# A decoder block on one core: seven block products for three quarters of the second MLP product, and another order of the first values

## The chip, the cores and the metric

The kernel runs on one core of one Trainium2 chip. The metric is the device time of one execution in microseconds, the median of several runs. A profile comes from one further execution, taken by the hardware profiler.

The engines are named as in the profile: PE is TensorE's matmul, PEld its weight load, DVE is VectorE, ACT is ScalarE, POOL is GpSimd, and SP is SyncE, whose queue issues nearly all DMAs of this kernel, in program order.

## The reference, cut to what matters

One decoder block over 1024 tokens of width 1024: a token mixer (retention and dilated attention), then an MLP. Both are behind an RMS norm that is modulated by a conditioning vector, and a last RMS norm follows. All values are fp32.

```
mod = silu(c) @ w_ada + b_ada;  sh1, sc1, g1, sh2, sc2, g2 = split(mod, 6)
h = rms_norm(x, norm1_g) * (1 + sc1) + sh1
x = x + g1 * token_mixer(h, ...)
h = rms_norm(x, norm2_g) * (1 + sc2) + sh2
x = x + g2 * (square(relu(h @ w_ff1)) @ w_ff2)          # 1024 -> 4096 -> 1024
out = rms_norm(x, norm_f_g)
```

The change touches the last line but one, in its second product (`w_ff2`, 4096 x 1024), and the first use of `h`, in the first projection of the token mixer (the attention values, `w_av`).

## The kernel before

Features stand on the 128 partitions and tokens in the free dimension. `x1` is eight tiles of 128 x 1024 (`G["x1", f]`), and the squared activations of the MLP are 32 such tiles, called `a` here and `a_d` in DRAM.

**Numbers.** Each fp32 operand is split into a high part, rounded to fp32r by ScalarE, and a low part, the difference, by VectorE. A product of two such pairs is three matmuls of 128 x 128 by 128 x 512 (`mm3`, lines 193, 195 and 197).

**Steps.** The class `Steps` (line 55) keeps a list of bodies, each with the weight tiles that it loads. Three raw buffers (tag `raw`) are loaded ahead on SP; `split_w` (line 180) makes the high and low parts into the tags `wh` and `wl`, three buffers each. A step that isn't `manual` has the weights of the next steps prepared ahead of its body; a manual one calls `ahead(...)` where it wants that. Loads beyond a mark wait for `first["release"]()`. The order of instructions on each engine is the order of the program.

**The first values.** `av_first` (line 768) runs over the eight k-tiles of `h`. PE needs `hh[k]` and `hl[k]`, the high and low parts. They come from `xt[k]` by VectorE's scaling (`h1_scale`, line 456), ScalarE's `hh` (line 458) and VectorE's `hl` (`h1_low`, line 461); ahead of the scaling, two rows of `w_ada` are multiplied with the condition on VectorE (`mod1`, line 433). One weight tile serves two k-tiles; for an even k, `ahead(1)` stands between the scaling and `mod1`, and has ScalarE round the next weight (line 183) and VectorE subtract (line 184). `split_first` (line 759) keeps the subtraction back in a list, to be called later; it was used for the first weight only.

**The first MLP product.** `ff1` (line 1642) makes 16 column blocks q of 256 features each by seven products for eight (class `Blocks`, line 212, items in the order 11, s1, s3, s2, 12, 22, s4, 12 matmuls each). Weight sums and splits (`prep`) run ahead as far as there are free slots: four of tag `g1` and four of `att` are used once, then four of `att` and six of `wh` and `wl` in turn. `post` forms the outputs on VectorE, and `f_out` (line 1609) applies relu and square on ScalarE and stores two tiles of `a` per block to DRAM (line 1622).

**The second MLP product.** `ff2(c, j)` (line 1759) runs over seven chunks c of four k-tiles each (512 of the 4096 features), and within a chunk over four weight tiles j. Each step does two column tiles f, each with two token halves: 24 matmuls into two PSUM banks. VectorE then adds the result, times the gate, to `x1` (line 1768). The k-tiles of `a` come back from DRAM through the raw buffers and are split ahead of their chunk (`a_prep`, lines 1754 and 1755). The eighth chunk is `ff2_last` (line 1785), in three runs over tokens, with the last norm and the output woven in. `x1` itself is loaded back from DRAM during the last column block of `ff1` and just behind it (`x1_load`, line 1508).

Of the kernel before, what the change touches and what calls it, by code (L numbers as in the profile page):

```python
# [11 lines left out]
F32 = mybir.dt.float32  # L12
F32R = mybir.dt.float32r
# [4 lines left out]
P = 128  # L18
# [114 lines left out]
def block_kernel(ctx, tc, io, stop=None, dbg=None):  # L133
# [34 lines left out]
    a1 = cst.tile([P, NK], F32, name="a1")  # L168
    a2 = cst.tile([P, NK], F32, name="a2")
    dsh = cst.tile([P, NK // 2], F32, name="dsh")  # L170
    ident = ct[:, CS_ID:CS_ID + P]
    ones = ct[:, CS_ONE:CS_ONE + 1]
    mhalf = ct[:, CS_MH:CS_MH + 8]
# [552 lines left out]
    def wsplit(ap):  # L726
        return ap, split_w
# [40 lines left out]
    def av_first(kk):  # L768

        def body(ahead, w):  # L770
            for k in (2 * kk, 2 * kk + 1):
                if k == 0:
                    for j, rb in enumerate(first["rb"]):
                        nc.scalar.copy(rb1[:, 512 * j:512 * j + 512], rb)
                if k + 1 < NK:
                    h1_mods(k + 1)
                    h1_scale(k + 1)
                    if k % 2 == 0:
                        ahead(1)
                    if k + 2 < NK:  # L780
                        mod1(k + 2)
                    h1_low(k + 1)
                av_k(0, k, w)
                if k == 3:
                    first["release"]()
                if k == 4:
                    for g in range(3):
                        bias_out(g)
                if k == NK - 1:
                    ahead(1)  # L790
                    nc.sync.dma_start(cs, io["cossin"])
                    nc.sync.dma_start(decay, io["decay"])
        return body
# [146 lines left out]
        new_head(0)  # L940

    for kk in range(4):
        steps.add(av_first(kk), [(io["w_av"][kk], split_w if kk else split_first)], manual=True)
    for g in (1, 2):
        for kk in range(4):
            steps.add(av_step(g, kk), [wsplit(io["w_av"][4 * g + kk])])
    steps.mark()
    steps.add(queries_keys, manual=True)

# [631 lines left out]

    M = {}
    NQ = DFF // 256
    a_d = [dram.tile([P, S], F32, name=f"ad{t}") for t in range(2 * NQ)]
    def w1_load(q, part):

        if q < 2:
# [21 lines left out]
    def f_out(q, n, x, y=None):  # L1609

        if ("out", q) not in M:
            M["out", q] = [G["p"].tile([P, S], F32, tag="g0", bufs=8, name=f"a{2 * q + i}") for i in range(2)]
        i, t = int(n[0]) - 1, int(n[1]) - 1
        o = M["out", q][i][:, 512 * t:512 * t + 512]
        if y is None:
            nc.scalar.activation(o, x, AF.Relu)
        else:
            (nc.vector.tensor_add if n == "12" else nc.vector.tensor_sub)(o, x, y)  # L1618
            nc.scalar.activation(o, o, AF.Relu)  # L1619
        nc.scalar.activation(o, o, AF.Square)  # L1620
        if n in ("12", "21"):
            nc.sync.dma_start(a_d[2 * q + i], M["out", q][i])
# [19 lines left out]
    def ff1(ahead):  # L1642
        def t_(k, half):
            return G["x1", k][:, 512 * half:512 * half + 512]

        def norm(k):
            t = t_(k, 1)
            nc.vector.scalar_tensor_tensor(t, t, a2[:, k:k + 1], G["rb"], op0=ALU.mult, op1=ALU.mult)

        banks(True)  # L1650

        BF.mm(0, "11", range(3))
        G["rs"] = rstd_rows(G["acc", "n21"], "n21", G["mp"], lambda: BF.prep((2, "11"), (2, "s1")))
# [60 lines left out]
        BF.post(1, "s2")  # L1714
        low()
        low = t4(2)
        l = t4(3)
        low()
        l()
        for k in range(NK):  # L1720
            del G["x1", k]
        for q in (3, 4):
            for part in (1, 2):
                w1_load(q, part)
        for q in range(2):
            BF.post(q, "12")
        sums = [(q, n) for q in range(2, NQ) for n in ORDER]
        items = [(q, n) for n in ("s4", "22") for q in range(2)] + sums

        def before(q, n):  # L1730
            if q == NQ - 2 and n == "s4":
                first["release"]()
            if q > 2 and n == ORDER[0] and q + 2 < NQ:
                for part in (1, 2):
                    w1_load(q + 2, part)
            if q == NQ - 1 and n in ("s2", "12"):
                for f in range(3):
                    x1_load(f + 3 * (n == "12"), x1_d)

        def after(q, n):  # L1740
# [5 lines left out]
        x1_load(7, x1_d)  # L1746

    def a_prep(t):

        def prep(raw):  # L1750
            pool, tag = ((G["p"], "g1"), (A["r1"], "att"))[t // 4 % 2]
            hi = pool.tile([P, S], F32R, tag=tag, bufs=8, name=f"a{t}h")
            lo = pool.tile([P, S], F32R, tag=tag, bufs=8, name=f"a{t}l")
# [89 lines left out]

    nff = DFF // P
    steps.add(ff1, manual=True)
    behind = [(a_d[t], a_prep(t)) for t in range(4)]
    for c in range(7):
        for j in range(4):
            steps.add(ff2(c, j), [wsplit(io["w_ff2"][4 * c + j])] + behind)
            behind = [(a_d[4 * c + 4 + j], a_prep(4 * c + 4 + j))]  # L1850
    for r in range(3):
        for j in range(4):
            steps.add(ff2_last(r, j), behind + [(io["w_ff2"][28 + j], last_prep(j))] if r == 0 else [])
            behind = []

    steps.run(startup)
# [17 lines left out]
def _k4(w):  # L1874

    k = w.shape[0]
    t = w.reshape(k // 512, 4, P, 4, 2, P).transpose(0, 3, 2, 4, 1, 5)
    return np.ascontiguousarray(t).reshape(k // 512 * 4, P, 1024)

def _vcols(w, width):  # L1880

# [44 lines left out]
def pack(x, c, w_ada, b_ada, norm1_g, w_in, rel_bias, ret_gn_g, ret_gn_b,  # L1926
# [27 lines left out]
        "w_ff2": _k4(A(w_ff2)[0]),  # L1954
    }
    a.update(_constants())
    return a
# [17 lines left out]
```

## Time and profile before

| | before |
|---|---|
| median of 3 runs | 2317.35 us (2315.91 to 2317.53) |
| the profiled execution | 2316.94 us |
| its span, first to last instruction | 2315.0 us |
| PE busy | 2261.9 us, 98%, 10466 matmuls |
| VectorE busy | 1350.1 us, 58% |
| ScalarE busy | 808.2 us, 35% |
| mean granted clock of PE | 0.998 |
| moved by DMA | 274.65 MB, mean 119 GB/s |

The profiled execution lies 0.41 us below the median, and its time is 1.94 us longer than its span. In the order of the span, the first values run from about 23 to 78 us, `ff1` from about 1626 to 1946, the seven chunks of `ff2` to about 2257, and the last chunk with the output to 2315. Matmuls are pipelined, so one has a duration of some 0.39 us while the next starts 0.23 us later; paces are therefore taken from start to start.

### The profile page before, as it was taken

How to read it: one execution, taken by the hardware profiler on the slowest of the kernel's cores; microseconds unless marked ns; L12 is line 12 of the kernel's file. 1: busy time of each engine (PE TensorE's matmuls, PEld its weight loads, DVE VectorE, ACT ScalarE, POOL GpSimd, SP SyncE). 2: the span in 40 equal slices, each digit the busy share in tenths (PEclk: the TensorE clock that was granted, in tenths of full speed). 3: DMA queues.
4: the chain of work that ended last, by engine and by line, in shares of the span. 5: the costliest groups of instructions: out<-in, count | busy, mean ns of one | idle time of the engine just before them, and what ended most of it. 6: DMA issues, size and time to landing. Idle time of an engine off the chain costs nothing.

```text
span 2315.0 us, 26666 instructions
## 1 busy us (share of the span) xinstructions
PE 2261.9 (98%) x10466; PEld 1864.6 (81%) x10466; DVE 1350.1 (58%) x1986; ACT 808.2 (35%) x1479; POOL 171.7 (7%) x136
## 2 busy tenths in 40 slices
PE   6999999999999999999999999999999999999998
PEld 4787888888878787888788888888778887888887
DVE  5626555547677676855555646567855554544445
ACT  3324233222334343444535411134454444221112
POOL 0000000001101010100000014401000000000003
PEclk9999999999999999999999999999999999999999
DMA  8532333332323232233323353253223336323222
GB/s 350 192 127 99 115 114 110 110 133 104 118 86 126 89 119 91 83 130 102 96 72 96 136 174 97 90 189 118 68 108 109 109 108 218 111 91 103 98 82 73
DMA packets 101661, 274.65 MB, mean 119 GB/s; under 512 B 22423, under 2 KB 33950, under 8 KB 101407
## 3 DMA queue, kind: packets, MB, share of 16 engines
q1 hardware_dynamic: 100382, 270.85, 34.1%
q0 software_dynamic: 1152, 2.10, 0.3%
q8 instruction: 82, 1.34, 0.2%
q14 instruction: 45, 0.36, 0.1%
HBM read 208.27 MB, written 67.00 MB: 119 GB/s over the span
## 4 chain that ended last, share of the span: by engine, by line
PE 57%; DVE 5%; ACT 3%; DMA 1%; issue 1%; POOLq 0%; SPq 0%; POOL 0%; DVEq 0%; ACTq 0%
PE f L193 4%; PE f L197 4%; PE f L195 4%; PE fp L193 4%; PE fp L197 4%; PE fp L195 4%; PE ro L195 3%; PE ro L193 3%; PE ro L197 3%; PE ak L193 2%; PE ak L195 2%; PE ak L197 2%; PE rg L195 1%; PE rg L193 1%; PE wo L193 1%; PE wo L195 1%
## 5 line engine op out<-in xcount | busy, mean ns | idle before, releaser
L1768 DVE SCALAR_TENSOR_TENSOR x1r<-f,mods,x1r 128x512 f32<-128x512 f32 x112 | 78.7, 746 | 153.4 <-PE f L197 153.4
L1479 POOL TENSOR_TENSOR g<-g,rt 128x1024 f32<-128x1024 f32 x24 | 66.2, 2760 | 432.2 <-DVE rt L1478 432.2
L193 PE MATMUL qap<-hh,qaw 128*128 128x512 f32 x216 | 84.3, 390 | 3.4 <-DVE qat L277 1.7
L197 PE MATMUL qap<-hh,qaw 128*128 128x512 f32 x216 | 84.1, 389 | 0.0
L195 PE MATMUL qap<-hl,qaw 128*128 128x512 f32 x216 | 84.0, 389 | 0.0
L1478 DVE TENSOR_TENSOR rt<-ro,g 128x1024 f32<-128x1024 f32 x32 | 39.0, 1219 | 57.4 <-PE ro L197 45.2
L555 POOL TENSOR_TENSOR j<-qk,j 128x512 fp32r<-128x512 f32 x32 | 44.0, 1374 | 364.0 <-ACT j L554 364.0
L1619 ACT ACTIVATE a<-a 128x512 f32<-128x512 f32 x48 | 30.4, 633 | 110.1 <-DVE a L1618 110.1
L1521 POOL TENSOR_TENSOR accnf<-accnf,sqnf 128x256 f32<-128x256 f32 (+1 forms) x18 | 16.6, 924 | 654.5 <-ACT sqnf L1520 654.5
L250 DVE TENSOR_TENSOR qaw<-wa,qaw 128x512 fp32r<-128x512 f32 x54 | 36.7, 689 | 39.5 <-ACT qaw L240 39.5
L1109 ACT ACTIVATE P<-P,ng 128x128 f32<-128x128 f32 (+1 forms) x96 | 41.9, 438 | 40.1 <-DVE ng L1106 40.1
L250 DVE TENSOR_TENSOR fw<-w1r,fw 128x512 fp32r<-128x512 f32 x48 | 32.8, 688 | 36.2 <-ACT fw L240 36.2
L193 PE MATMUL fp<-h2h,fw 128*128 128x512 f32 x128 | 50.6, 395 | 0.5 <-ACT ft2nsq L272 0.5
L193 PEld LDWEIGHTS qap<-hh,qaw 128*128 128x128 f32 x216 | 40.5, 188 | 12.6 <-DVE qat L277 2.2
L197 PE MATMUL fp<-h2h,fw 128*128 128x512 f32 x128 | 50.3, 393 | 0.0
L195 PE MATMUL fp<-h2l,fw 128*128 128x512 f32 x128 | 50.2, 392 | 0.0
L633 ACT CAST vh<-v 128x512 fp32r<-128x512 f32 x32 | 18.8, 588 | 89.3 <-PE v L597 87.2
L575 ACT COPY sm<-sT 128x128 f32<-128x128 f32 x32 | 8.5, 267 | 113.9 <-PE sT L566 113.9
L197 PEld LDWEIGHTS qap<-hh,qaw 128*128 128x128 f32 x216 | 40.5, 188 | 8.5
L195 PEld LDWEIGHTS qap<-hl,qaw 128*128 128x128 f32 x216 | 40.5, 188 | 8.3
L240 ACT CAST qaw<-wa 128x512 fp32r<-128x512 f32 x54 | 32.5, 616 | 36.1 <-PE qap L197 36.1
L438 DVE SCALAR_TENSOR_TENSOR raw<-raw,cb 128x1024 f32<-128x1024 f32 x32 | 43.3, 1354 | 0.0
(3521 smaller groups left out, 6943.5 us busy)
## 6 DMA issues: line engine op xcount, KB each, us to landing
raw<-in_w_ada_dram SPq DMA_DIRECT2D x32, 512.0 KB, 3.5
w1r<-in_w_ff_dram SPq DMA_DIRECT2D x32, 512.0 KB, 5.2
ad<-a SPq DMA_DIRECT2D x32, 512.0 KB, 3.0
raw<-in_w_ff_dram SPq DMA_DIRECT2D x32, 512.0 KB, 3.5
raw<-ad SPq DMA_DIRECT2D x32, 512.0 KB, 4.4
em<-in_w_ada_dram SPq DMA_DIRECT2D x16, 512.0 KB, 10.2
qkd<-qa SPq DMA_DIRECT2D x16, 512.0 KB, 2.6
raw<-in_w_rv_dram SPq DMA_DIRECT2D x16, 512.0 KB, 4.4
```

The lines of the kernel that those rows point to most:

```text
L193: nc.tensor.matmul(o, wl, xh, start=first, stop=False, skip_group_check=skip)
L195: nc.tensor.matmul(o, wh, xl, start=False, stop=False, skip_group_check=skip)
L197: nc.tensor.matmul(o, wh, xh, start=False, stop=last, skip_group_check=skip)
L240: nc.scalar.copy(t[:, :512], src)
L250: nc.vector.tensor_sub(t[:, 512:], src, fv(t[:, :512]))
L438: nc.vector.scalar_tensor_tensor(raw, raw, 1.0, cb, op0=ALU.mult, op1=ALU.mult, accum_out=mods[:, i:i + 1])
L555: nc.gpsimd.tensor_sub(t[:, 1], src, fv(t[:, 0]))
L1109: nc.scalar.activation(v, v, AF.Exp, bias=ng[:, blk:blk + 1], accum_out=st[:, g, blk, 2 + a:3 + a])
L1478: nc.vector.tensor_mul(t, flat(ps), sg)
L1479: (nc.vector if h == H - 1 else nc.gpsimd).tensor_add(m, m, t)
L1619: nc.scalar.activation(o, o, AF.Relu)
L1768: nc.vector.scalar_tensor_tensor(x, ps[hf], mods[:, G2 + i:G2 + i + 1], x, op0=ALU.mult, op1=ALU.add)
```

## The change

Two things are changed.

First, `av_first`: the next weight's rounding on ScalarE is issued ahead of the k-tile's own work, all its weights (and the first one of the next step) keep their low part back, and that subtraction and `h1_low` now stand ahead of `mod1` of the tile after next; for odd k, `h1_low` stands between the two multiplications of `mod1`.

Second, the second MLP product. Its first 24 k-tiles (3072 of 4096 features) are three chunks of eight k-tiles. In a chunk the matrix of activations is seen as 2 x 2 blocks (even and odd k-tiles by two token halves) and that of weights too (even and odd k-tiles by even and odd column tiles). A product of such matrices is made by seven products of sums of blocks. The sums of activations are formed in `ff1` by `a_sums` (four VectorE instructions per column block, q 0 to 11) and stored in seven slots of `xs_d`. The sums of weights are formed by `b_w`, on VectorE. `PLAN` lists per product the slot of x, the set of PSUM banks (a, b or c), the block of the output to which the set belongs after this product, and the sign. A set isn't cleared between products: it keeps the sum, and after each product it is added to another block of `x1` (`b_post`). Each product runs over four pairs p of column tiles, one bank each. Weights and x are made two products ahead (`b_w(i + 2, p)`, `b_x(i + 2, ...)`), x is loaded three ahead (`b_load(i + 3)`); the raw weights are loaded into buffers of the tags `raw`, `rl`, `wh` and `wl` (`RAWS`). The first loads and splits are made in the last column block of `ff1` (`second_ahead`). The seventh chunk of the old form (k-tiles 24 to 27) and `ff2_last` stay.

Two of the four slots of tag `att` in `ff1` are now used once (`att*`), and `a_sums` takes their buffers. The host lays out the first 3072 rows of `w_ff2` another way (`_quads`). The diff, cut to its core:

```diff
@@ av_first
+                if k % 2 == 0:
+                    ahead(1)
                 if k + 1 < NK:
                     h1_mods(k + 1)
                     h1_scale(k + 1)
-                    if k % 2 == 0:
-                        ahead(1)
-                    if k + 2 < NK:
-                        mod1(k + 2)
-                    h1_low(k + 1)
+                    if first["lows"]:
+                        first["lows"].pop(0)()
+                        h1_low(k + 1)
+                        if k + 2 < NK:
+                            mod1(k + 2)
+                    elif k + 2 < NK:
+                        mod1(k + 2, (SC1,))
+                        h1_low(k + 1)
+                        mod1(k + 2, (SH1,))
+                    else:
+                        h1_low(k + 1)
...
-        steps.add(av_first(kk), [(io["w_av"][kk], split_w if kk else split_first)], manual=True)
+        steps.add(av_first(kk), [(io["w_av"][kk], split_first)], manual=True)
...
@@ f_out
         if n in ("12", "21"):
-            nc.sync.dma_start(a_d[2 * q + i], M["out", q][i])
+            r = M["out", q][i]
+            if q >= 4 * NS:                                    # NS = 3
+                nc.sync.dma_start(a_d[2 * q + i], r)
+            elif i == 0:
+                nc.sync.dma_start(xs_d[q // 4][:, 0, q % 4], r[:, :512])
+            else:
+                nc.sync.dma_start(xs_d[q // 4][:, 1:3, q % 4], r.rearrange("p (t x) -> p t x", t=2))
+    def a_sums(q, part):
+        e, o = M["out", q]
+        r = A["r1"].tile([P, 2, 512], F32, tag="att", bufs=8, name=f"as{q}{part}")
+        if part == 0:
+            nc.vector.tensor_sub(r[:, 0], e[:, :512], e[:, 512:])
+            nc.vector.scalar_tensor_tensor(r[:, 1], r[:, 0], -1.0, o[:, 512:], op0=ALU.mult, op1=ALU.subtract)
+            M["t2", q] = r[:, 1]
+        else:
+            nc.vector.tensor_sub(r[:, 0], o[:, 512:], e[:, 512:])
+            nc.vector.scalar_tensor_tensor(r[:, 1], M.pop(("t2", q)), -1.0, o[:, :512], op0=ALU.mult,
+                                           op1=ALU.subtract)
+        nc.sync.dma_start(xs_d[q // 4][:, 3 + 2 * part:5 + 2 * part, q % 4], r)
-    BF = Blocks("f", X, ["g1"] * 4 + ["att*"] * 4 + ["att"] * 4 + ["wh", "wl"] * 3,
+    BF = Blocks("f", X, ["g1"] * 4 + ["att*"] * 4 + ["att"] * 2 + ["att*"] * 2 + ["wh", "wl"] * 3,
@@ ff1
-            if q == NQ - 2 and n == "s4":
-                first["release"]()
...
         def after(q, n):
-            if q == NQ - 1 and n == "12":
-                ahead()
+            if (q, n) == (2, "11"):
+                todo.extend((p, part) for p in range(2) for part in range(2))
+            elif n == "11" and 2 < q <= 4 * NS:
+                todo.extend((q - 1, part) for part in range(2))
+            if todo and (q, n) != (1, "22"):
+                a_sums(*todo.pop(0))
+            if q == NQ - 1:
+                second_ahead(n)
...
+        b_x(1, 0)
+        b_x(1, 1)
+    PLAN = {"11": (0, "a", "11", 1), "s1": (3, "c", "22", -1), "s2": (4, "a", "12", 1), "s4": (2, "c", "12", 1),
+            "s3": (5, "a", "22", -1), "12": (1, "b", "11", 1), "22": (6, "a", "21", -1)}
+    SEQ = [(c, n) for c in range(NS) for n in PLAN]
...
+    def b_split(hi, lo, src):
+        nc.scalar.copy(hi, src)
+        b_flush()                       # the low part of the split before
+        B["low"].append((lo, src, hi))
+    def b_load(i):                      # x of product i: two loads of 512 KB, into the tiles of the low parts
...
+    def b_w(i, p):
...
+        if n == "s1":
+            B["s", p] = G["mh"].tile([P, 512], F32, tag="mh", bufs=32, name=f"w2s{c}{p}")
+        if n == "s3":
+            src = b21
+            nc.vector.tensor_add(src, b21, b11)
+        elif n[0] == "s":
+            src = B["s", p]
+            nc.vector.tensor_add(src, *{"s1": (b21, b22), "s2": (src, b11), "s4": (src, b12)}[n])
+        else:
+            src = {"11": b11, "12": b12, "22": b22}[n]
+        hi, lo = mh(f"w2h{i}{p}"), mh(f"w2l{i}{p}")
+        b_split(hi, lo, src)
+        B["w", i, p] = hi, lo
+    def b_mm(i, p):
+        c, n = SEQ[i]
+        bank = PLAN[n][1]
+        if n in ("11", "s1", "12"):
+            B["ps", bank, p] = ps_s(f"f2{bank}{i}{p}")
+        ps, (wh, wl) = B["ps", bank, p], B["w", i, p]
+        for m in range(4):
+            mm3([ps], (wh[:, m * P:m * P + P], wl[:, m * P:m * P + P]), [B["x", i, m // 2][m % 2]],
+                m == 0 and n in ("11", "s1", "12"), m == 3, True)
+    def b_post(i, p):
+        _, bank, (r, t), sign = PLAN[SEQ[i][1]]
+        f = 2 * p + int(r) - 1
+        x = G["x1", f][:, 512 * (int(t) - 1):512 * int(t)]
+        g = mods[:, G2 + f:G2 + f + 1] if sign > 0 else ng2[:, f:f + 1]
+        nc.vector.scalar_tensor_tensor(x, B["ps", bank, p], g, x, op0=ALU.mult, op1=ALU.add)
+    def second_ahead(n):
+        if n == "11":
+            nc.vector.tensor_scalar_mul(ng2, mods[:, G2:G2 + NK], -1.0)
+            for s in range(2):
+                b_raw(0, "11", s)
+            b_load(0)
+            b_raw(0, "21", 0)
+        elif n == "s1":
+            b_raw(0, "21", 1)
+            b_raw(0, "22", 0)
+            for p in range(4):
+                b_w(0, p)
+        elif n == "s3":
+            b_raw(0, "22", 1)
+            b_x(0, 0)
+            b_x(0, 1)
+        elif n == "12":
+            for p in range(4):
+                b_w(1, p)
+        elif n == "22":
+            b_load(1)
+    def ff2_blocks(ahead):
+        for i, (c, n) in enumerate(SEQ):
+            if i == 0:
+                b_load(2)
+                for s in range(2):
+                    b_raw(0, "12", s)
+            if i + 3 < len(SEQ) + 2:
+                b_load(i + 3)
+            if c + 1 < NS:
+                for b in {"s3": ("11", "21"), "12": ("12",), "22": ("22",)}.get(n, ()):
+                    for s in range(2):
+                        b_raw(c + 1, b, s)
+            if i == len(SEQ) - 2:
+                first["release"]()
+            for p in range(4):
+                b_mm(i, p)
+                if i + 2 < len(SEQ):
+                    b_w(i + 2, p)
+                if p % 2 == 0 and i + 2 < len(SEQ) + 2:
+                    b_x(i + 2, p // 2)
+                if B["post"]:
+                    b_post(*B["post"].pop())
+                B["post"].append((i, p))
+                if i == len(SEQ) - 1 and p == 1:
+                    b_flush()
+                    ahead(1)
+        b_flush()
+        b_post(*B["post"].pop())
...
     steps.add(ff1, manual=True)
-    behind = [(a_d[t], a_prep(t)) for t in range(4)]
-    for c in range(7):
+    steps.add(ff2_blocks, manual=True)
+    behind = []
+    for c in range(2 * NS, 7):
```

More of the change, by code (lines that the diff above doesn't have):

```diff
@@ L170, in block_kernel @@
     dsh = cst.tile([P, NK // 2], F32, name="dsh")
+    ng2 = cst.tile([P, NK], F32, name="ng2")
     ident = ct[:, CS_ID:CS_ID + P]
@@ L790, in body @@
                     ahead(1)
+                    if first["lows"]:
+                        first["lows"].pop(0)()
                     nc.sync.dma_start(cs, io["cossin"])
@@ L1583, in block_kernel @@
     NQ = DFF // 256
-    a_d = [dram.tile([P, S], F32, name=f"ad{t}") for t in range(2 * NQ)]
+    NS = 3
+    a_d = {t: dram.tile([P, S], F32, name=f"ad{t}") for t in range(8 * NS, 2 * NQ)}
+    xs_d = [dram.tile([P, 7, 4, 512], F32, name=f"xsd{c}") for c in range(NS)]
     def w1_load(q, part):
@@ L1746, in ff1 @@
         x1_load(7, x1_d)
+        b_x(1, 0)
[3 more added lines that the diff above has]
+    SEQ = [(c, n) for c in range(NS) for n in PLAN]
+    RAWS = [dict(zip(("11", "21", "22", "12"), t)) for t in
+            (("raw raw", "raw rl", "rl wh", "wl wh"), ("wl wl", "wh raw", "raw raw", "rl rl"),
+             ("wh wh", "wl wl", "wl wh", "rl rl"))]
@@ new lines, in block_kernel, with b_tiles, b_raw @@
+    B = {"low": [], "ps": {}, "post": []}
+    def b_tiles(name):
+        return (G["p"].tile([P, S], F32R, tag="g1", bufs=8, name=name + "h"),
+                A["r1"].tile([P, S], F32R, tag="att", bufs=8, name=name + "l"))
+    def b_raw(c, b, s):
+        tag = RAWS[c][b].split()[s]
+        pool = {"raw": wraw, "rl": G["mp"]}.get(tag, whl)
+        t = pool.tile([P, 1024], F32, tag=tag, bufs=2 if tag == "rl" else 3, name=f"w2r{c}{b}{s}")
+        nc.sync.dma_start(t, io["w_ff2s"][(4 * c + ("11", "12", "21", "22").index(b)) * 2 + s])
+        B[c, b, s] = t
@@ new lines, in b_flush @@
+    def b_flush():
+        if B["low"]:
+            lo, src, hi = B["low"].pop()
+            nc.vector.tensor_sub(lo, src, fv(hi))
+    def b_split(hi, lo, src):
[3 more added lines that the diff above has]
+    def b_load(i):
+        for j in range(2):
+            if i < len(SEQ):
+                c, n = SEQ[i]
+                src = xs_d[c][:, PLAN[n][0], 2 * j:2 * j + 2].rearrange("p m x -> p (m x)")
+            else:
+                src = a_d[8 * NS + 2 * (i - len(SEQ)) + j]
+            lo = A["r1"].tile([P, S], F32R, tag="att", bufs=8, name=f"b{i}{j}l")
+            nc.sync.dma_start(fv(lo), src)
+            B["x", i, j] = lo
@@ new lines, in b_x @@
+    def b_x(i, j):
+        lo = B["x", i, j]
+        hi = G["p"].tile([P, S], F32R, tag="g1", bufs=8, name=f"b{i}{j}h")
+        b_split(hi, lo, fv(lo))
+        if i < len(SEQ):
+            B["x", i, j] = [(hi[:, 512 * m:512 * m + 512], lo[:, 512 * m:512 * m + 512]) for m in range(2)]
+        else:
+            M["a", 8 * NS + 2 * (i - len(SEQ)) + j] = hi, lo
+    def b_w(i, p):
+        c, n = SEQ[i]
+        b11, b12, b21, b22 = (B[c, b, p // 2][:, 512 * (p % 2):512 * (p % 2) + 512] if (c, b, p // 2) in B else None
+                              for b in ("11", "12", "21", "22"))
+        if n == "s1":
[6 more added lines that the diff above has]
+            nc.vector.tensor_add(src, *{"s1": (b21, b22), "s2": (src, b11), "s4": (src, b12)}[n])
+        else:
+            src = {"11": b11, "12": b12, "22": b22}[n]
+        hi, lo = mh(f"w2h{i}{p}"), mh(f"w2l{i}{p}")
+        b_split(hi, lo, src)
+        B["w", i, p] = hi, lo
@@ L1852, in block_kernel @@
         for j in range(4):
-            steps.add(ff2_last(r, j), behind + [(io["w_ff2"][28 + j], last_prep(j))] if r == 0 else [])
+            steps.add(ff2_last(r, j), behind + [(io["w_ff2"][28 - 8 * NS + j], last_prep(j))] if r == 0 else [])
             behind = []
```

17 lines of the change are left out of this document (11 added, 6 removed).

## The prediction

> **What bounds the kernel now.** I read the page first, then busy time by stretch, then the instructions of TensorE and VectorE in order of time at the two places that the change touches. The page says who is full:
>
> ```profile
> PE 2261.9 (98%) x10466; PEld 1864.6 (81%) x10466; DVE 1350.1 (58%) x1986; ACT 808.2 (35%) x1479; POOL 171.7 (7%) x136
> ```
>
> Busy time by stretch (PE, PEld, DVE, ACT, POOL, then granted clock, DMA share, GB/s) shows it for the first MLP product (first row) and the second (last row):
>
> ```profile
> 1860.00:1900.00 40.00, 40.00 (x175) 32.57 (x175) 21.21 (x33) 18.44 (x32) 0.00 (x0) 1.00 0.29 105
> ...
> 2050.00:2100.00 50.00, 50.00 (x220) 41.05 (x219) 23.10 (x28) 8.10 (x8) 0.00 (x0) 1.00 0.33 106
> ```
>
> And finer, the one place between them where PE ran dry, and what the clock did next:
>
> ```profile
> 1646.00:1650.00 4.00, 2.62 (x11) 1.40 (x9) 3.93 (x7) 2.52 (x4) 0.00 (x0) 1.00 0.00 0
> 1650.00:1654.00 4.00, 2.91 (x9) 2.13 (x8) 3.96 (x6) 1.24 (x2) 0.00 (x0) 0.73 0.00 0
> ```
>
> So a matmul removed from the second product is worth its full pace, as long as VectorE (DVE), which had half its time free there, keeps up. The pace is read from two VectorE events that follow PE: the updates of x1 come in pairs, every 24 matmuls (three such intervals lie between these two rows), and `ft6nsq`, `ft7nsq` stand one column block (84 matmuls) apart:
>
> ```profile
> 2064.16 1.41 DVE L1768 SCALAR_TENSOR_TENSOR x1r<-f,mods,x1r 128x512 f32<-128x512 f32 x2 [1.82 <-PE f L197]
> ...
> 2080.64 0.75 DVE L1768 SCALAR_TENSOR_TENSOR x1r<-f,mods,x1r 128x512 f32<-128x512 f32 x1 [4.08 <-PE f L197]
> ```
> ```profile
> 1764.29 0.69 DVE L276 TENSOR_TENSOR ft6nsq<-ft6nsq,fp 128x512 f32<-128x512 f32 x1 [1.40 <-PE fp L197]
> ...
> 1771.17 0.68 DVE L235 TENSOR_TENSOR fs<-w1r 128x512 f32<-128x512 f32 x1
> 1773.13 0.69 DVE L250 TENSOR_TENSOR fw8s<-fs,fw8s 128x512 fp32r<-128x512 f32 x1 [1.28 <-ACT fw8s L240]
> ...
> 1783.70 0.69 DVE L276 TENSOR_TENSOR ft7nsq<-ft7nsq,fp 128x512 f32<-128x512 f32 x1 [1.40 <-PE fp L197]
> ```
>
> So 72 matmuls in 16.48 us are 228.9 ns each in the plain product; 84 in 19.41 us are 231.1 ns in the block form, 12 to a bank. The two middle rows of the second fence matter later: from the sum of a weight to its low part 1.96 us pass, because ScalarE's rounding lies between.
>
> At the start, in the order of time, VectorE sets the pace and PE waits (first VectorE, then PE):
>
> ```profile
> 56.08 1.29 DVE L456 SCALAR_TENSOR_TENSOR xt<-xt,a,rb 128x1024 f32<-128x1024 f32 x1
> 59.52 1.23 DVE L184 TENSOR_TENSOR raw_510l<-raw,raw_510h 128x1024 fp32r<-128x1024 f32 x1 [2.15 <-ACT raw_510h L183]
> ```
> ```profile
> 50.89 2.12 PE L750 MATMUL av<-raw_282h,hl 128*128 128x512 f32 x8 [1.33 <-DVE hl L461]
> 53.59 0.50 PE L750 MATMUL av<-raw_294l,hh 128*128 128x512 f32 x1 [0.58 <-ACT hh L458]
> ```
>
> **The matmuls.** The first 24 of 32 k-tiles cost 24 x 8 column tiles x 2 token halves x 3 passes = 1152 matmuls; by seven products for eight they cost 3 x 7 x 4 pairs x 12 = 1008. Before: 1152 x 228.9 ns = 263.7 us, and the waits at the start of the product: first matmul at 1946.38, last update of the 1344 at 2257.1, so 310.7 us less 307.6 is 3.1 us; together 266.8. After: the products have the block form, 1008 x 231.1 ns = 233.0 us (230.7 at the other pace). So 33.8 us go if nothing waits. In sentences apart: the Trainium skill ("TensorE: Matmul & The Clock Gate", section "Wait — 56ns, not 53.3ns?") gives 215.7 ns from start to start for 512 columns. The trace says 6 to 7% more, and the measurement decides; by the page's figure the 144 matmuls would be 31.1 us.
>
> **VectorE under the products.** A product lasts 48 x 231.1 ns = 11.09 us on PE. In it VectorE does four low parts of weights (start to start 0.61 us), two of x (128x1024, 1.14), four additions from PSUM to x1 (0.66 to 0.75, the L1768 rows; say 0.70), and for four products in seven four weight sums (0.61): 9.96 us with sums, 7.52 without. The 1.96 us chain is filled by an earlier low part except twice in a product, some 0.74 each: 11.4 with sums. Over seven: 4 x 11.4 + 3 x 7.5 = 68.1 against 77.6 on PE. It lies beside PE, with 12% to spare; within the run of four sums VectorE falls back about 0.3 us a product, and weights and x are made two products ahead, so a lag up to about one product costs nothing. PSUM: a bank set is used again two products later, the addition comes one pair (2.8 us) after its matmuls; hidden likewise. ScalarE: 4 x 0.61 + 2 x 1.04 = 4.5 us of 11.09.
>
> **Sums of the activations, in the first product.** Per column block two subtractions (0.69) and two fused ones (0.75): 2.9 us for 12 blocks of 16, on a VectorE that has 10.4 of 19.4 us in use; 13.3 after. The cover is its idle time, 1.40 us ahead of `ft7nsq` and more in each item. Not so in the first block after the start, q=2: there PE already waited 1.69 us for `ft2h2t`, and four such steps (5.8 us) now come ahead of it, while two kept weight slots fewer put off two weights (2.6 us). I take 2 us of new wait, between 0 and 4. Stores grow from 1.05 to 1.84 MB a block, some 95 GB/s, with 105 GB/s moved now and 410 seen at the start.
>
> **What is moved on the queues.** Each product issues two x loads on SP, which wait for the low parts of the product before; the next chunk's raw weights stand behind them. Those of block 22 are asked for in the same product in which the first sum uses them; they land some 5 us after its start, VectorE stands still about 7 us, and its lag at the end of that product is 6 us of the 11 allowed: free, by some 4 us. At the beginning the cover is thinner: the loads of x1 tiles 6 and 7 wait for the stores of the last block and then hold SP; in the trace they were issued 12 us after the second product began:
>
> ```profile
> 1955.19 1.50 SPq L1622 DMA_DIRECT2D ad<-a  x2
> 1958.52 1.55 SPq L1508 DMA_DIRECT2D x1r<-x1d  x2
> ```
>
> The third product's x and block 12 queue behind these. VectorE was held by other waits there, so I expect them 3 to 5 us earlier, landed at 13 to 16 us, with the x needed at 22: a wait of 0 to 4. For both places and the last block (where additions wait behind the first weights) I take 3 us. Together with q=2 that is 5 us of new waits, from 0 to 18. The release of the next weights, moved from block 14 to the last products but one, has two products (22 us) to load 512 KB, landing 3.5 us after issue; `ng2` is one small instruction.
>
> **The start.** For two k-tiles VectorE needs 13.4 us (46.13 to 59.52), of which 2.15 wait for ScalarE's rounding of the weight; PE needs 48 x 231 ns = 11.08. With the rounding issued first, its low part fits where VectorE would wait for `hh`, and the low part of h comes before two weight products. VectorE then needs 11.24 per pair. Laying out the rows again from 28.92 us, PE waits 0.7, 0.25 and 0.25 us instead of 7.4 in all between 31.82 and the last k-tile's end at 78.1: 6.2 saved; 5.7 with a little for each handover, from 3 to 6.3. The raws land in time: the fourth, issued at 41.29, landing 9.8 later, at 51.1, is rounded from there, and the `hh` behind it is due at 53.
>
> **Sum.** 266.8 - (233.0 + 5) = 28.8, and 5.7: 34.5 us. The profiled execution took 2316.94 (span 2315.0, 1.94 around it) and becomes 2282.4; the median of the three, 2317.35, stands 0.4 above it: 2282.9.
>
> **Rivals.** First, slower: VectorE becomes the bound of the products. It decides once a product needs over (266.8 + 5.7) / 21 = 13.0 us of VectorE, against the 9.7 above. The trace has such a row, the same kind of subtraction in the last stage:
>
> ```profile
> L1781 DVE TENSOR_TENSOR wll<-raw,wlh 128x512 fp32r<-128x512 f32 x8 | 6.6, 865 | 2.5 <-ACT wlh L1780 2.5
> ```
>
> At 865 ns for each 128x512, a product with sums takes 12 x 0.865 + 4 x 0.865 + 1.5 = 15.3 us, one without 10.4, three chunks 277 us, 10 over the 266.8, less 5.7 from the start: 2322. Against it: POOL worked beside that row and has nothing to do under the products. Second, the feed is late: at the beginning and at both chunk changes a load costs PE 5 us beyond the cover, and the clock drops as at 1650 (0.73 over 4 us, 1.1 us): 18 us in place of 5, so 2295.9. For it: 8 weights and 14 x tiles per chunk, in order, on one queue that stands at each wait; against it: 22 x 0.52 MB in 77.6 us are 149 GB/s. The Trainium skill (same page, "HAM oscillation — how this bites in real kernels") warns of idle gaps over about 3.4 us, after which the clock falls to half. The rows at 1646 to 1654 agree in kind, with 0.73 over a window; by the rule each such wait would cost 1.7 us more, 5 in all. Third, the start buys nothing, because `hh`, not the low parts, comes last: 2288.6.
>
> **How the numbers follow.** Forecast 0.67, late feed 0.18, no gain at the start 0.10, VectorE as the bound 0.05. Low end: no new wait, the faster pace, all of the start: 36.1 + 6.3, so 2275. High end: the late feed, 2296. Over 0.2% (4.6 us, about what a measurement of this kernel can tell): faster 0.94, the same 0.01, slower 0.05.
>
> **What would show it.** PE 144 instructions fewer; products 11.1 us apart with no PE wait but at their beginning; VectorE near 40 of 50 us under them, with x1 additions of 0.74 us; the first k-tiles ending near 72 instead of 78; block q=2 waiting 3 to 4 us. Wrong would be: PE waits inside the runs of sums (VectorE), or at each seventh product (feed), or a pace far from 231 ns.

## The result, and the profile after

| | device time, median | lowest to highest | profiled execution / span |
|---|---|---|---|
| before | 2316.89 us | 2315.21 to 2318.24 | 2316.94 / 2315.0 us |
| changed | 2309.36 us | 2308.70 to 2312.01 | 2308.90 / 2306.9 us |
| predicted | 2282.9 us | 2275 to 2296 | |

The ratio is 0.997, with an interval of 0.9961 to 0.9979: 7.5 us faster, where 34.5 were forecast. The direction was right, but the median lies 26.5 us above the predicted time. The first line of the page of the changed kernel shows that the work left as planned; PE has 144 instructions fewer:

```profile
PE 2240.7 (97%) x10322; PEld 1837.1 (80%) x10322; DVE 1446.1 (63%) x2149; ACT 849.7 (37%) x1557; POOL 171.5 (7%) x136
```

PE's busy time fell by 21.2 us, where 144 matmuls at 228.9 ns are 33.0, and its share fell too. To find where the rest stayed, take a few instructions that both kernels have and compare when they start (us; the last two columns are the lead over the kernel before; the very last belongs to `e12_no_shift`, a kernel that comes at the end of the experiments):

| start of | before | changed | lead | lead, `e12_no_shift` |
|---|---|---|---|---|
| first copy of `avo` | 76.6 | 71.1 | 5.5 | 5.9 |
| first update of x behind the output projection | 1543.3 | 1540.5 | 2.8 | 4.4 |
| `ft2nsq` (first product, block 2) | 1688.0 | 1689.3 | -1.3 | 4.1 |
| `ft12nsq` | 1880.3 | 1901.2 | -20.9 | 1.8 |
| first matmul of the second product | 1946.4 | 1968.1 | -21.7 | 0.2 |
| first matmul of its last row (`f2l`) | 2256.5 | 2248.7 | 7.8 | 34.5 |
| end of the span | 2315.0 | 2306.9 | 8.1 | 34.0 |

The second product itself took 280.5 instead of 310.1 us, so it delivered 29.5. Most of the loss lies ahead of it: 19.6 us between `ft2nsq` and `ft12nsq`, in ten blocks of the *first* product, 4.1 just before, and 2.7 in steps that the change doesn't touch.

Busy time by stretch (its length, then PE, PEld, DVE, ACT, POOL, granted clock, DMA share, GB/s): one block of the first product, the place ahead of the first product where PE ran dry before too, and the products.

```profile
1795.30:1816.50 21.20, 19.48 (x84) 15.69 (x84) 12.93 (x22) 9.31 (x16) 0.00 (x0) 1.00 0.39 137
...
1646.00:1650.00 4.00, 2.45 (x8) 1.72 (x9) 3.93 (x7) 1.13 (x3) 0.00 (x0) 0.91 0.00 0
1650.00:1654.00 4.00, 4.00 (x13) 3.12 (x13) 3.93 (x7) 1.18 (x2) 0.00 (x0) 0.66 0.19 50
...
1975.20:2205.00 229.80, 229.72 (x984) 183.95 (x983) 182.75 (x250) 90.52 (x124) 0.00 (x0) 1.00 0.47 157
```

A block lasts 21.2 us instead of 19.4, and PE is idle 1.7 of them. The products run almost without a gap (PE 229.72 of 229.80 us), VectorE 80% busy. VectorE in order of time, the block from `ft6nsq` to `ft7nsq` and the end of the next:

```profile
1778.07 0.69 DVE L251 TENSOR_TENSOR fw<-w1r,fw 128x512 fp32r<-128x512 f32 x1 [1.87 <-ACT fw L241]
1779.74 0.69 DVE L251 TENSOR_TENSOR fw<-w1r,fw 128x512 fp32r<-128x512 f32 x1 [0.98 <-ACT fw L241]
...
1786.06 0.69 DVE L251 TENSOR_TENSOR fw<-w1r,fw 128x512 fp32r<-128x512 f32 x1 [1.87 <-ACT fw L241]
1786.67 0.68 DVE L1651 TENSOR_TENSOR as<-a 128x512 f32<-128x512 f32 x1
1787.39 0.69 DVE L1652 SCALAR_TENSOR_TENSOR as<-as,a 128x512 f32<-128x512 f32 x1
1788.00 0.68 DVE L236 TENSOR_TENSOR fs<-w1r 128x512 f32<-128x512 f32 x1
1789.37 0.69 DVE L251 TENSOR_TENSOR fw8s<-fs,fw8s 128x512 fp32r<-128x512 f32 x1 [0.69 <-ACT fw8s L241]
1789.98 0.69 DVE L1655 TENSOR_TENSOR as<-a,a 128x512 f32<-128x512 f32 x1
1790.58 0.69 DVE L1656 SCALAR_TENSOR_TENSOR as<-as,a 128x512 f32<-128x512 f32 x1
1791.18 0.68 DVE L236 TENSOR_TENSOR fs<-w1r,w1r 128x512 f32<-128x512 f32 x1
...
1795.26 0.68 DVE L277 TENSOR_TENSOR ft7nsq<-ft7nsq,fp 128x512 f32<-128x512 f32 x1
...
1816.45 0.68 DVE L277 TENSOR_TENSOR ft8nsq<-ft8nsq,fp 128x512 f32<-128x512 f32 x1
```

Before, `ft7nsq` came after 1.40 us of waiting for PE. Now no wait stands there: VectorE arrives late and PE waits for it, as the waits of PE show (total, times, longest):

```profile
PE fp L194 <- DVE ft2h2t L278: 6.4, 1, 6.4
...
PE fp L194 <- DVE ft8h2t L278: 1.7, 1, 1.7
...
PE fp L194 <- DVE ft15h2t L278: 1.1, 1, 1.1
```

All other idle times of VectorE in these rows end with ACT (ScalarE), and such waits are still there. At the start, in the order of time (VectorE, then PE), the low part of the weight now follows without its 2.15 us of waiting, and what is left of PE's waits there is for `hh`:

```profile
53.73 1.22 DVE L764 TENSOR_TENSOR raw_490l<-raw,raw_490h 128x1024 fp32r<-128x1024 f32 x1
...
49.75 0.50 PE L751 MATMUL av<-raw_274l,hh 128*128 128x512 f32 x1 [0.56 <-ACT hh L459]
```

Under the products PE's pace is not the 228.9 to 231.1 ns of the prediction. These two rows are 17 matmuls apart, 233 ns each, with no wait listed between (233.3 ns over the 30 us from 2000 on):

```profile
2042.63 0.39 PE L198 MATMUL f2a<-b60h,w2h 128*128 128x512 f32 x1
...
2046.59 0.40 PE L196 MATMUL f2a<-b61l,w2h 128*128 128x512 f32 x1
```

### The profile page after: what moved, and what is told of

Same layout as the page of the kernel before. It is cut to its first block, busy times and chain, and to the rows that moved or that the text cites. A ratio compares the mean times of both kernels' runs of the same rounds, so it can differ in the third digit from the quotient of the medians.

```text
span 2306.9 us, 26766 instructions
## 1 busy us (share of the span) xinstructions
PE 2240.7 (97%) x10322; PEld 1837.1 (80%) x10322; DVE 1446.1 (63%) x2149; ACT 849.7 (37%) x1557; POOL 171.5 (7%) x136
## 4 chain that ended last, share of the span: by engine, by line
PE 77%; DVE 12%; ACT 6%; issue 2%; DMA 1%; SPq 0%; DVEq 0%; POOLq 0%; POOL 0%; ACTq 0%
PE qap L194 5%; PE qap L198 5%; PE qap L196 5%; PE av L751 4%; PE ro L194 3%; PE ro L196 3%; PE ro L198 3%; PE rg L194 3%; PE rg L196 3%; PE rg L198 3%; PE v L596 2%; PE ak L194 2%; PE v L598 2%; PE v L597 2%; PE ak L196 2%
## 5 line engine op out<-in xcount | busy, mean ns | idle before, releaser
L1533 POOL TENSOR_TENSOR accnf<-accnf,sqnf 128x256 f32<-128x256 f32 (+1 forms) x18 | 16.5, 919 | 649.9 <-ACT sqnf L1532 649.9
L1823 ACT CAST w2h<-w2s 128x512 fp32r<-128x512 f32 x36 | 22.4, 621 | 80.2 <-DVE w2s L1861 78.4
L194 PE MATMUL fp<-xt,fw 128*128 128x512 f32 x64 | 27.2, 425 | 21.7 <-DVE ft2h2t L278 6.4
```

The source lines that it names most:

```text
L194: nc.tensor.matmul(o, wl, xh, start=first, stop=False, skip_group_check=skip)
```

## The experiments

Theory A: the four `a_sums` instructions lengthen a chain of VectorE and ScalarE, each waiting for the other, that runs through the whole block. Rivals: B, the two weight slots fewer; C, the longer stores. Theory D: the new tile `ng2` (32 bytes per partition) sits below everything else on the left side of SBUF and moves those tiles, and the distance between a matmul's two operands sets its pace. All ratios are to the kernel before, timed beside each kernel.

**Leave out the sums; undo the slots.** `e1_no_sums`:

```diff
-        r = A["r1"].tile([P, 2, 512], F32, tag="att", bufs=8, name=f"as{q}{part}")
-        ...  (the four subtractions)
+        r = (e, o)[part].rearrange("p (t x) -> p t x", t=2)
```

> The changed kernel with the VectorE arithmetic of the sums left out: `a_sums` stores the same number of bytes to the same places straight from the activation tiles, and the four subtractions per block are not done (so the products of the second MLP product run on other numbers, at the same cost). Weight slots, loads, stores and everything else stay. Theory A (the four instructions lengthen VectorE's serial chain with ScalarE in each block of the first MLP product, 19.4 to 21.2 us in ten blocks, and 4.7 us at block 2): the blocks return to 19.4 us, the waits behind `ft..h2t` disappear, and the kernel takes 2309 - 10 x 1.78 - 4.7 - 1 = 2285 us (2283 to 2288). Theory B (the two weight slots fewer cause it) or C (the longer stores and their queue cause it): the blocks stay at 21.2 us and the kernel at 2309 us (2306 to 2310).

2289.54 us, ratio 0.9884 (0.987 to 0.9897). A holds, C falls: the same stores, and 19.8 us gone. `ft7nsq` waits for PE again:

```profile
1784.06 0.69 DVE L277 TENSOR_TENSOR ft7nsq<-ft7nsq,fp 128x512 f32<-128x512 f32 x1 [0.72 <-PE fp L198]
...
1803.29 0.69 DVE L277 TENSOR_TENSOR ft8nsq<-ft8nsq,fp 128x512 f32<-128x512 f32 x1 [0.54 <-PE fp L198]
```

It missed the expected 2285 (2283 to 2288): PE still waits 2.5 us for `ft2h2t`, and blocks 13 to 15, which never had sums, gave nothing back. `e2_slots`, on the kernel before:

```diff
-    BF = Blocks("f", X, ["g1"] * 4 + ["att*"] * 4 + ["att"] * 4 + ["wh", "wl"] * 3,
+    BF = Blocks("f", X, ["g1"] * 4 + ["att*"] * 4 + ["att"] * 2 + ["att*"] * 2 + ["wh", "wl"] * 3,
```

> The kernel before with one part of the change: only two of the four `att` weight slots are kept in the first MLP product, the other two are used once. Theory B (slots): the blocks of the first MLP product lengthen from 19.4 to about 21.2 us, so 2317 + 18 to 23 = 2335 to 2340 us. Theory A (sums on VectorE): no change of the blocks, 2317 us (2315 to 2319).

2317.66 us, ratio 1.0007 (0.9998 to 1.0016). B falls as a cause by itself: from `ft3nsq` on the blocks keep their 19.3 us. But the slots take half of VectorE's room in a block, 0.66 us where it was 1.40:

```profile
1787.57 0.69 DVE L276 TENSOR_TENSOR ft7nsq<-ft7nsq,fp 128x512 f32<-128x512 f32 x1 [0.66 <-PE fp L197]
```

It is the room that the kernel without sums has too. What the sums would cost with all four slots kept, no run shows.

**The same sums, put where VectorE waits.** `e5_sums_in_gaps` calls `a_sums` between `prep` and `flush`, that is between ScalarE's rounding and the low part that waits for it:

```diff
                     self.prep(sums.pop(0))
+                mid(q, n)
                 self.flush()
...
+        def mid(q, n):
+            at = {(0, "22"): (0, 0), (2, "11"): (0, 1)}.get((q, n))
+            if q >= 2 and n == "12":
+                at = q - 1, 0
+            elif q >= 3 and n == "11":
+                at = q - 2, 1
+            if at and at[0] < 4 * NS:
+                a_sums(*at)
```

> The changed kernel with the same four instructions of `a_sums` per block, issued elsewhere: part 0 of block q-1 in item 12 of block q and part 1 in item 11 of block q+1, both between `prep` and `flush`, where VectorE stood idle for 1.87 us waiting for ScalarE's rounding. Theory A in its sharper form (the place in VectorE's serial chain costs, not the work): VectorE does 1.3 us in each of two idle times of 1.87 us, the blocks return to 19.4 us, and the kernel comes to the time of the one without sums, 2289.5 us (2288 to 2292). Rival (VectorE has too much to do in this stage wherever the sums stand): the blocks stay near 21.2 us and the kernel at 2305 to 2309 us.

2290.19 us, ratio 0.9882 (0.9869 to 0.9896): nothing was left out, and it takes what the kernel without sums takes. VectorE in order of time:

```profile
1784.40 0.69 DVE L1635 TENSOR_TENSOR a<-ft7h2t,fp 128x512 f32<-128x512 f32 x1
1785.01 0.68 DVE L1652 TENSOR_TENSOR as<-a 128x512 f32<-128x512 f32 x1
1785.72 0.69 DVE L1653 SCALAR_TENSOR_TENSOR as<-as,a 128x512 f32<-128x512 f32 x1
1786.96 0.69 DVE L251 TENSOR_TENSOR fw<-w1r,fw 128x512 fp32r<-128x512 f32 x1 [0.55 <-ACT fw L241]
...
1802.18 0.69 DVE L277 TENSOR_TENSOR ft8nsq<-ft8nsq,fp 128x512 f32<-128x512 f32 x1 [0.53 <-PE fp L198]
```

From the subtraction that begins the item (first row) to the low part it is 2.56 us, as in the changed kernel (1796.69 to 1799.25); the idle time between shrank from 1.87 to 0.55 us. Within what these runs can tell, the sums themselves cost nothing; their place did.

**The start alone.** `e7_start_alone` makes the changed kernel's edits of lines 774 to 960 in the kernel before, without `ng2`.

> The kernel before with only the reordered start (order of `ahead`, `mod1` and `h1_low` in the first values, and the low parts with it); nothing else, and no `ng2`. By the step of the prediction that the profile of the changed kernel bore out (first activations copy 5.5 us earlier): 2316.1 - 5.5 = 2310.6 us (2309.5 to 2311.5), all of it kept to the end because no address moves. Rival (the unchanged stages give 2.7 us back whatever the addresses, since each of them has a pace of its own): 2313.3 us.

2311.49 us, ratio 0.9975 (0.9965 to 0.9985): 5.8 us, all of it kept to the end. So the middle steps don't give back time by themselves; the 2.7 us in the changed kernel have another cause.

**Move the addresses and nothing else.** On the kernel before:

```diff
     dsh = cst.tile([P, NK // 2], F32, name="dsh")
+    pad = cst.tile([P, NK], F32, name="pad")          # e3: 32 bytes; e8: 2 * NK, 64 bytes
+    nc.vector.memset(pad, 0.0)
```

> The kernel before with one dead tile of 32 bytes per partition added to the pool of constants (and one memset of it), which moves every pool on the left side of SBUF by 32 bytes as the new `ng2` does and changes nothing else. Theory D (a matmul whose weights and moving operand stand in different classes of address modulo 64 bytes takes 233.3 instead of 228.9 ns): the attention and output steps lose the 2.7 us that they lost in the changed kernel, and the 1152 matmuls of the second MLP product that pair left weights with right moving operands lose up to 1152 x 4.4 ns = 5 us each way: 2320 to 2327 us. If addresses do not matter: 2317 us (2315.5 to 2318.5).

2325.89 us, ratio 1.0041 (1.0029 to 1.0054). A dead tile of 32 bytes costs 9.8 us; between the first copy of `avo` and the first update of x it loses 2.9 us, about the 2.7 of the changed kernel. The stretch from 2040 to 2080 us (PE busy and its matmuls, granted clock, DMA share, GB/s) lies in the plain second product; first before, then with the dead tile:

```profile
2040.00:2080.00 40.00, 40.00 (x177) 1.00 0.33 105
```
```profile
2040.00:2080.00 40.00, 40.00 (x173) 1.00 0.26 85
```

PE is full in both and does 177 or 173 matmuls. On the changed kernel, `ng2` widened from 32 to 64 bytes (`cst.tile([P, 2 * NK], ...)[:, :NK]`), first alone, then with the sums in the gaps:

> The changed kernel with `ng2` taken from a tile of twice its width (64 bytes per partition, half of it unused), so that the pools on the left stand modulo 64 bytes as they did in the kernel before. Theory D (addresses modulo 64 set the pace of a matmul whose weights and moving operand stand on different sides): the unchanged stretch up to 1543 us gets its 2.7 us back, and the 1008 matmuls of the products go from 233 towards 229 ns, about 4 us, with 2 us more in the 384 plain ones behind them: 2299 to 2303 us. If the 9.8 us that the 32-byte tile cost in the kernel before came from something else than the addresses: 2309 us (2307.5 to 2310.5).

2298.77 us, ratio 0.9919 (0.9905 to 0.9932): 10.6 us won, a little more than expected.

> Both together: sums in VectorE's idle times, and `ng2` from a tile of 64 bytes. If A and D are two independent losses, their gains add: 2289.5 - 8 = 2281 us (2279 to 2284), about what was predicted for the change. If the shift of addresses was hidden or does not matter: 2289 us.

2273.65 us, ratio 0.9816 (0.9802 to 0.9829). Here the wider tile won 16.5 us, and the kernel is well below the expected range. The two gains don't just add. With the sums in VectorE's chain PE can't use a better pace in the first product, as it waits there anyway: from `ft2nsq` to `ft15nsq` the wider tile won 0.5 us with the old place of the sums (271.7 to 271.2) and 3.9 with the new one (254.7 to 250.8). That is 3.4 of the 5.9 us between the two gains; the rest was not followed. Again two rows of the products, 17 matmuls apart, now 226.5 ns each (226.7 over 30 us):

```profile
2042.72 0.39 PE L196 MATMUL f2a<-b91l,w2h 128*128 128x512 f32 x1
...
2046.57 0.39 PE L194 MATMUL f2a<-b90h,w2l 128*128 128x512 f32 x1
```

That is better than the 228.9 ns of the kernel before, which the theory as first put (only distances modulo 64 bytes, that is the remainders of the two addresses on division by 64) doesn't allow. Four more layouts: the dead tile of 64 bytes in the kernel before (its edit stands above); in the changed kernel with the sums in the gaps, a dead tile on the right side, and `ng2` from a tile of `6 * NK` (192 bytes) or `4 * NK` (128 bytes).

> The kernel before with one dead tile of 64 bytes per partition in the pool of constants (and a memset of it), nothing else. Three paces were seen in steady stretches: 226.7 ns from one matmul's start to the next's with 64 bytes added on the left, 228.9 to 229.2 ns with nothing added, 233.3 ns with 32 bytes added. Modulo 128 bytes the tiles on the right stand at 96, those on the left at 96, 32 and 64 in these three cases. Theory D2 (the distance modulo 128 bytes between weights and moving operand sets the pace: 0 is best, 64 next, 32 worst): 1152 matmuls of the second MLP product, some 1344 of the first and some 960 of the steps from 1326 to 1543 us win 2.2 to 2.5 ns each, so 2317 - 8 = 2309 us (2307 to 2312). Theory D1 (only the distance modulo 64 counts; the 226.7 ns come from the changed kernel's other order): 2317 us (2315.5 to 2318.5).

2309.48 us, ratio 0.9965 (0.9952 to 0.9977): 8.4 us for a tile that nothing reads.

> The changed kernel with the sums in VectorE's idle times (2290.2 us) and `ng2` at its 32 bytes, with a dead tile of 32 bytes put at the outer end of the right side, so that the pools on both sides are shifted: left and right both stand at 64 modulo 128. If the distance between the two operands counts (D1 and D2): 2273.7 us (2272 to 2277), the time of the variant with 64 bytes on the left. If the left side's own address counts (64 modulo 128 is bad wherever the other operand stands): 2290 us.

```diff
+    rpad = ctx.enter_context(tc.tile_pool(name="rpad", bufs=1, side="right")).tile([P, NK], F32, name="rpad")
+    nc.vector.memset(rpad, 0.0)
```

2273.13 us, ratio 0.9812 (0.9799 to 0.9825). The left stands at the very addresses of the 2290 us kernel; moving the right side by the same 32 bytes gives all of it back. So it is the distance between the two sides that counts.

> The changed kernel with the sums in VectorE's idle times and `ng2` from a tile of 192 bytes: left and right both at 96 modulo 128, but 128 bytes apart modulo 256 (with 64 bytes they agreed modulo 256 too). D2 (distance modulo 128): 2273.7 us (2272 to 2277). If the distance modulo 256 counts: between 2278 and 2290 us.

2288.76 us, ratio 0.9876 (0.9863 to 0.989).

> The changed kernel with the sums in VectorE's idle times and `ng2` from a tile of 128 bytes: left at 32, right at 96 modulo 128, as in the kernel before; equal modulo 64. D2: a pace of 229 ns, between the other two: 2273.7 + some 3450 matmuls x 2.3 ns = 2281.5 us (2279 to 2284). D1 (distance modulo 64 only): 2273.7 us.

2288.45 us, ratio 0.9878 (0.9863 to 0.9893). Both readings fall by these two: modulo 64 both layouts are equal, modulo 128 the first of them is, and neither is fast. What all layouts together show (addresses as the compiled programs allocate them, the left side with the weights of the second product, the right with its moving operand; the distance is left less right; pace from start to start in that product):

| left, right modulo 256 | distance | pace | kernels |
|---|---|---|---|
| 224, 224 and 192, 192 | 0 | 226.7 ns | e4, e6, e8, e9 |
| 160, 224 | 192 | 228.9 ns | before, e7, e12 |
| 96, 224 | 128 | 232.3 ns | e10 |
| 32, 224 | 64 | 233.3 ns | e11 |
| 192, 224 | 224 | 233.3 ns | changed, e1, e3, e5 |

Equal modulo 256 is best; no simple rule orders the others. The two best layouts are also equal modulo 512, so whether 256 is enough wasn't settled. Moving one operand's tiles alone wasn't tried either. The mechanism stays open.

**Both causes removed, every address as before.** `e12_no_shift` is `e5_sums_in_gaps` with

```diff
-    ng2 = cst.tile([P, NK], F32, name="ng2")
+    ng2 = a1
```

> The changed kernel with the sums in VectorE's idle times, and `ng2` without a tile of its own: it takes the place of `a1`, which is not read after the first values. No pool moves, so all addresses are those of the kernel before (left 160, right 224 modulo 256). If the two causes, sums in VectorE's chain and the shift by 32 bytes, are all that was missing in the prediction's sum, this kernel should take what was predicted for the change, 2282.9 us; from the runs: the kernel before got 8.4 us faster by equal addresses, so 2273.7 + 8.4 = 2282 us (2280 to 2284.5). If some third loss hides behind them, or the shift costs only together with `ng2`: 2286 us or more, or 2274 us.

2281.42 us, ratio 0.9839 (0.9825 to 0.9852). This is the change with its sums where they cost nothing, on the addresses from which the prediction's durations were read: 1.5 us below the predicted time. PE's two largest single waits in the two products:

```profile
PE fp L194 <- DVE ft2h2t L278: 2.7, 1, 2.7
...
PE fp L194 <- DVE ft15h2t L278: 1.3, 1, 1.3
```

The best kernels are those with the sums in the gaps and the two operands equal modulo 256, 2273.1 and 2273.7 us: 36 us under the changed kernel, 44 under the one before.

## Why the prediction was wrong

**The step that failed: the sums of the activations, in the first product.** "The cover is its idle time, 1.40 us ahead of `ft7nsq` and more in each item." An engine's idle time covers added work only where what it waits for comes no later because of that work. The 1.40 us ended with PE, and that was all the room there was; the two slots fewer had already taken half of it (0.66 in `e2_slots`), which the prediction put into block 2 alone. The "more in each item" (1.87, 0.98, 1.27, ...) ended with ScalarE, and ScalarE had been started by VectorE: an addition (or the subtraction of an output) on VectorE, ScalarE's rounding behind it, a low part on VectorE, and the next addition only then. Work put between two such links moves the later link, and the wait behind it stays as long as it was. In the rows of the changed kernel, part 0 puts 1.94 us between a low part and the next addition (1786.06 to 1788.00), part 1 1.81 (1789.37 to 1791.18); where no sums stand between, as in `e1_no_sums`, it is 0.61. That is 2.5 us a block. Without sums VectorE had 0.7 us to spare, so 1.8 us were to be lost, and a block went from 19.4 to 21.2. Block 2 waited 6.4 us, where 3 to 4 were expected. With it the place of the sums cost 2309.4 - 2290.2 = 19.2 us of the 26.5. The prediction had the two rows of this chain in its own fence, said that the 1.96 us between them matter later, and used them only for the products.

The Trainium skill ("Perfetto Trace Analysis", section "Identifying the Most-Contended Engine") looks for the bottleneck by occupancy and calls it, for VectorE, a fair measure of how close one is to roofline. As a sign of room for more work it misleads here: VectorE was 61% busy (12.93 of 21.20 us) in the stretch in which its chain set the pace, and 80% busy under the products, where it did not.

**A term that was missing: the addresses.** "`ng2` is one small instruction" counted its instruction and not its 32 bytes. They cost 2290.19 - 2281.42 = 8.8 us. (19.2 and 8.8 are 28.0: the 26.5 that were missing, and the 1.5 by which `e12_no_shift` is below the prediction.) The tile also broke the assumption under every other term, that rows of the kernel before hold in the changed one: the products took 235.7 us where the sum had 233.0, and the middle steps gave back 2.7 us without a changed line. On the old addresses (`e12_no_shift`) the products took 231.8. The Trainium skill ("SBUF — State Buffer", section "Who interferes with whom") gives TensorE two independent read ports, one for the moving operand and one for weight loads, and says that it never waits on anyone for SBUF. If the two were independent in every respect, no distance should matter; the runs have 226.7 to 233.3 ns. Whether the ports are the cause, no run shows.

**What held.** The start: 5.5 us in the trace and 5.8 alone, against 5.7. That it fits is in part luck: PE's waits fell from 7.4 to 3.0 us, four waits of 0.55 to 1.24 for `hh`, and not to the 1.2 laid out, so the third rival's `hh` was partly there; but each wait that went also saved the slow restart around it, some 0.27 us (an estimate from start times: 0.16 before and 0.11 behind the wait at 49.75). The second product: the 144 matmuls went, and in `e12_no_shift` it lasted 275.7 instead of 310.1 us, 34.3 saved against a forecast of 33.8 less up to 3. New waits: the table's last column gives back 5.7 us between the start and the products, against 5; but 1.5 of these lie in unchanged steps, where that execution had a lower granted clock (0.97 from 1300 to 1350, 1.00 in `e7_start_alone`), so 4.2 belong to the change. VectorE as the bound of the products did not come: its additions from PSUM took this (minimum, median, maximum in ns),

```profile
L1883 DVE SCALAR_TENSOR_TENSOR x1r<-f2a,mods,x1r x24: 743/746/752, 1987.4 to 2163.1; 128x512 f32<-128x512 f32 x24
```

and its low parts 0.68 to 0.69 us, not the 0.865 of the rival's row. That row was a mean of unlike durations: its median is 0.68 us, and only the two pairs from 2264.10 on, while POOL was at work, took longer, up to 1.45. The late feed did not come either, though its transfers were late: x of the third product was issued 12.3 us after the products began, behind the second x1 load (not 3 to 5 us ahead of the 12 of before, as hoped), was there at 17 instead of 13 to 16, and was first used at 23. VectorE stood 7.1 us for block 22, as worked out. PE had no wait from either.

```profile
1974.32 5.98 SPq L1520 DMA_DIRECT2D x1r<-x1d  x2
1980.38 0.38 SPq L1837 DMA_DIRECT2D b20l<-xsd  x1
```
```profile
2042.89 0.69 DVE L1861 TENSOR_TENSOR w2s<-w2r,w2r 128x512 f32<-128x512 f32 x1 [7.09 <-DMA w2r<-in_w_ff2s_dram]
```

Two of the three named rivals were about the stage that gets faster, and the third about the start. What happened was in the stage that feeds the faster one, with a price that the text put at "2 us of new wait, between 0 and 4".

## What to carry to other kernels

Ask of every idle time that shall cover new work *who ends it, and who started that one*. If the chain leads back to the engine itself, the idle time is a link of the chain and covers only what is issued inside it, between the request and the wait. The true room of a block is the wait that ends with the engine that bounds it. And before comparing two kernels by their rows, compare where their operands stand: a new tile, however small, can move the tiles behind it.

## What the runs showed of the hardware

TensorE's pace on 128x512 matmuls, with a new weight each time and no wait, depended on the distance of the two operands' addresses: 226.7 ns where they agree modulo 256 bytes (here modulo 512 too), 228.9 to 233.3 ns where they don't, up to 2.9% more. A dead tile of 32 bytes made the kernel before 9.8 us slower, one of 64 bytes 8.4 us faster.

A wait of PE can cost more than its length. Behind the 2.7 us for `ft2h2t` in `e2_slots` the next matmuls started 0.43 us apart until 1696.70, fourteen of them, instead of 0.23; behind the 6.4 us in the changed kernel six did, and behind 2.5 us in `e5_sums_in_gaps` and 1.7 us in the kernel before none. The windows show it as a lower granted clock (0.66 from 1690 to 1700 in `e2_slots`). No long gap is needed: at the place where PE runs dry in the kernel before, matmuls were as slow from 1651.95 on, behind three waits of at most 1.1 us each.
